# Where ScalarE issues the split of h that returns from device memory: behind the newest weight set's high part

## The chip, the cores and the metric

One NeuronCore of one Trainium2 chip runs the kernel. The metric is device time in microseconds (us); smaller is better. The engines are PE (TensorE, matrix products), ACT (ScalarE), DVE (VectorE), POOL (GpSimd) and SP (SyncE, which here only issues transfers). PEld is PE's loading of stationary operands.

## The reference

Two layers act on x of 256 positions by 1024 channels. Each layer is a half-step SwiGLU block, a mixing block of 16 heads in four groups, and another half-step SwiGLU block. A last RMSNorm follows.

```python
def swiglu(x, w_gate, w_up, w_down):
    return (jax.nn.silu(x @ w_gate) * (x @ w_up)) @ w_down     # 1024 -> 2816 -> 1024
...
x = x + 0.5 * swiglu(rms_norm(x, norm_ffn1[l]), ...)
x = x + hybrid_mixer(rms_norm(x, norm_mix[l]), ...)
x = x + 0.5 * swiglu(rms_norm(x, norm_ffn2[l]), ...)
```

The change touches only the SwiGLU blocks, four in all (called FFN below). There h stands for the 2816 values silu(gate) * up of each position.

## The kernel before, in words

**Sets.** All weights pass through the kernel as "sets", 328 of them, in one list: two blocks of 128 rows by up to 512 columns, 512 KB. `Set.load` issues the transfer into `wraw` on SP's queue (L137) and then calls `split`, which makes two tiles from it: `whi`, the rounded high part, by one ACT instruction, and `wlo`, the rest, by one DVE instruction that reads `whi`. Both are called through the helper `keep`, so the profile puts them on L115. A product in near-float32 precision takes six matmuls for each set and half of the positions (`Set.mm`, L149): high by high, high by low and low by high, for each of the two blocks.

**Order of work.** The 256 positions are two halves, h=0 and h=1. `consume(h, i)` uses set i for half h. The half h=1 follows five sets behind (LAG = 5), so that the traced order is (0,i), (1,i-5), (0,i+1), (1,i-4), and so on; at the end of a block the five outstanding uses of h=1 run alone (L773). `consume(0, i)` first loads sets up to i+2 (AHEAD = 2), so `done[0] - 1`, the newest loaded set, is i+2 from then on. The tiles `whi` and `wlo` have eight buffers each (`wsp`), so ACT may make `whi` of set j only when both halves have used set j-8. The raw tiles have four buffers, and each comes free when `wlo` is made.

**One FFN block.** The 2816 columns are cut into 11 chunks c of 256. Chunk c takes four sets (`gate_up`, s = 0 to 3), whose last one ends in `sg` = silu(gate) * up (L318 on ACT, L319 on DVE). From chunk 2 on, the two sets of `down_` for chunk c-2 come behind the four of chunk c. So a period is six sets. `down_` needs h transposed (`hT`), again as a high and a low part, `hhi` and `hlo`.

**Two ways to transpose.** For chunks 0, 1 and 10 (NEAR), `turn` transposes on PE. For the other eight chunks, `turn_far` transposes 32x32 blocks on DVE (L298), writes them to device memory in four transfers (L301) and reads them back with the blocks exchanged (L305), both on POOL's queue. Two yields place these steps: the read is traced four `advance` calls after `sg`, and `split` of the returned tile `pT` ten more. `advance` is called once for each `consume`, so `split` is traced in the fourteenth call. There are 8 chunks x 2 halves x 4 blocks = 64 such splits.

**Who sets the order on an engine.** The kernel is traced in the order above, and a planner then lays each engine's instructions into one fixed order, by what it expects to be ready when. Each engine works off its own order, one instruction after the other. `tc.issue_after(x)` makes what is traced in its block on x's engine stand behind x in that order; it adds no wait for x to finish, and it does nothing to other engines.

The names that follow: `Set.load` (L129 to L140), `split` (L119), `keep` (L111), `turn_far` (L294 to L309), `gate_up` (L311), `down_` (L322), `consume` (L748).

Of the kernel before, what the change touches and what calls it, by code (L numbers as in the profile page):

```python
# [11 lines left out]
AF = mybir.ActivationFunctionType  # L12
# [43 lines left out]
def hybrid_kernel(ctx: ExitStack, tc: tile.TileContext, a: dict, out: bass.AP):  # L56
    nc = tc.nc
# [12 lines left out]
    def bank(tag):  # L70
        return ps.tile([P, 512], F32, name=f"ps_{tag}")

    def quad(tag):
        return ps.tile([P, 4, P], F32, name=f"ps_{tag}")
# [36 lines left out]
    def keep(engine, f, *args, **kw):  # L111

        last = fixed.get(engine)
        with tc.issue_after(last.ins) if last is not None else nullcontext():
            ins = f(*args, **kw)  # L115
        if engine in fixed:
            fixed[engine] = ins

    def split(pt, hi, lo):  # L119
        keep("ACT", nc.scalar.activation, hi, pt, AF.Copy)  # L120
        keep("DVE", nc.vector.tensor_tensor, lo, pt, hi.bitcast(F32), op=ALU.subtract)

    class Set:

# [4 lines left out]
        def load(self, parts=1):  # L129

            n = self.n
            r = raw.tile([P, 2, 512], F32, name="wraw")[:, :, :n]
            self.hi = wsp.tile([P, 2, 512], F32R, name="whi")[:, :, :n]
            self.lo = wsp.tile([P, 2, 512], F32R, name="wlo")[:, :, :n]
            ks = [slice(2 * i // parts, 2 * (i + 1) // parts) for i in range(parts)]
            for k in ks:
                self.dma = nc.sync.dma_start(r[:, k], self.src[:, k])  # L137
            for k in ks:
                yield
                split(r[:, k], self.hi[:, k], self.lo[:, k])  # L140

        def mm(self, acc, hi, lo, first, last):
            xs = ((hi, self.hi), (hi, self.lo), (lo, self.hi))
# [18 lines left out]
    sets = []  # L162
# [6 lines left out]
    def spawn(gen):  # L169

        wait = next(gen, None)
        if wait is not None:
            alive.append([gen, wait])
# [5 lines left out]
    def advance():  # L179
        for job in list(alive):  # L180
            job[1] -= 1
            if job[1] <= 0:
                job[1] = next(job[0], None)
                if job[1] is None:
                    alive.remove(job)
        for h in range(2):
            for job in list(running[h]):
                job[1] -= 1
                if job[1] <= 0:
                    job[1] = next(job[0], None)  # L190
                    if job[1] == 0:
                        job[2] = True
                        job[1] = next(job[0], None)
                    if job[1] is None:
                        running[h].remove(job)
            if lines[h] and all(j[2] for j in running[h]):
                gen = lines[h].pop(0)
                running[h].append([gen, next(gen), False])
# [4 lines left out]
    class Norm:  # L203
# [33 lines left out]
        def take_turned(self, h, c, xg, parts=1, on=nc.sync):  # L237


            xg = xg.rearrange("p (k t) -> p k t", t=P)  # L240
            self.parts[h, c] = hi, lo = tuple(big.tile([P, 4, P], F32R, name=f"x{t}{h}{c}") for t in ("hi", "lo"))
            n = 4 // parts
            ks = [slice(n * i, n * i + n) for i in range(parts)]
            for k in ks:
                on.dma_start(xg[:, k], a["xT"][h, c, :, k])
            for k in ks:
                yield
                g = gcol[:, 4 * c:4 * c + 4][:, k].unsqueeze(2).to_broadcast([P, n, P])
                keep("DVE", nc.vector.tensor_tensor, xg[:, k], xg[:, k], g, op=ALU.mult)
                split(xg[:, k], hi[:, k], lo[:, k])  # L250
# [7 lines left out]
        def turn(self, h, c, xg):  # L258
            yield TURN_X
            pt = quad("t")  # L260
            for j in range(4):
                nc.tensor.transpose(pt[:, j, :], xg[:, j * P:(j + 1) * P], ident)  # L262
            hi, lo = (big.tile([P, 4, P], F32R, name=f"x{t}{h}{c}") for t in ("hi", "lo"))
            split(pt, hi, lo)
            self.parts[h, c] = hi, lo
# [7 lines left out]
    def residual(h, c, acc, scale, nxt):  # L273
        n = 2 if nxt.final and h == 1 and c == 1 else 1
        w = 512 // n
        for i in range(n):
            xs = x[h][:, c * 512 + i * w:c * 512 + i * w + w]
            nc.vector.scalar_tensor_tensor(xs, acc[:, i * w:i * w + w], scale, xs, op0=ALU.mult, op1=ALU.add)
            nxt.take(h, c, i, n)

    def add_ffn(norm, gu, down, nxt):
        phases.append(len(sets))
        hT = {}
        acc = {}

        def turn(h, c, hh):
            yield 2 if h == 1 and c == 10 else TURN_H
            pt = quad("t")
            for j in range(2):
                nc.tensor.transpose(pt[:, j, :], hh[:, j * P:(j + 1) * P], ident)  # L290
            hT[h, c] = tuple(hbuf.tile([P, 2, P], F32R, name=f"h{t}{h}") for t in ("hi", "lo"))
            split(pt[:, :2, :], *hT[h, c])

        def turn_far(h, c, hh):  # L294


            st = work.tile([P, 512], F32, name="z")[:, :256]
            nc.vector.transpose(st, hh)  # L298
            far = dram.tile([4, 32, 4, 64], F32, name="far")
            for a_ in range(4):  # L300
                nc.gpsimd.dma_start(far[:, :, a_, :].rearrange("b j e -> j b e"),  # L301
                                    st[32 * a_:32 * a_ + 32].rearrange("j (b e) -> j b e", b=4))
            yield FAR
            back = work.tile([P, 4, P], F32, name="pT").rearrange("p a t -> p (a t)")[:, :256]
            nc.gpsimd.dma_start(back, far.rearrange("b j a e -> (b j) (a e)"))  # L305
            yield BACK
            back = back.rearrange("p (a k i) -> p k a i", a=4, k=2)
            hT[h, c] = tuple(hbuf.tile([P, 2, P], F32R, name=f"h{t}{h}") for t in ("hi", "lo"))
            split(back, *(t.rearrange("p k (a i) -> p k a i", a=4) for t in hT[h, c]))  # L309

        def gate_up(h, c, s, st):  # L311
            if s == 0:
                acc[h] = bank("g")
            st.mm(acc[h], *norm.blocks(h, (2 * s, 2 * s + 1)), s == 0, s == 3)
            if s == 3:
                sg = work.tile([P, 256], F32, name="sg")
                r = norm.scale[h]
                nc.scalar.activation(sg, acc[h][:, :256], AF.Silu, scale=r)  # L318
                nc.vector.scalar_tensor_tensor(sg, acc[h][:, 256:], r, sg, op0=ALU.mult, op1=ALU.mult)  # L319
                spawn((turn if c in NEAR else turn_far)(h, c, sg))  # L320

        def down_(h, c, d, st):  # L322
            if c == 0:
                acc[h, d] = bank(f"d{h}")
            while (h, c) not in hT:
                advance()
            hi, lo = hT[h, c]
            st.mm(acc[h, d], [hi[:, k, :] for k in range(2)], [lo[:, k, :] for k in range(2)], c == 0, c == 10)
            if c == 10:
                residual(h, d, acc[h, d], 0.5, nxt)  # L330

        def add_down(c):
            for d in range(2):
                sets.append(Set(down[c, d], 512, lambda h, st, d=d: down_(h, c, d, st)))

        for c in range(11):
            for s in range(4):
                sets.append(Set(gu[c, s], 512, lambda h, st, c=c, s=s: gate_up(h, c, s, st)))
            if c > 1:
                add_down(c - 2)  # L340
        add_down(9)
        add_down(10)
# [418 lines left out]
    done = [0]  # L761
# [98 lines left out]
```

## Time and profile before

| what | value |
|---|---|
| three runs | 1020.0, 1019.18, 1019.8 us; median 1019.8 us |
| the profiled execution | 1020.97 us, of which the span from first to last instruction is 1019.2 us |
| PE, PEld busy | 996.3 us, 801.4 us |
| DVE, ACT busy | 642.0 us, 515.8 us |
| POOL busy | 195.0 us |
| transfers | 200.36 MB, mean 197 GB/s |
| granted clock of PE over the span | 0.995 |

How to read it: an engine that is busy nearly all the time sets the pace, and then the time that can be won is the time in which it stands still. A matmul's record covers more than the interval to the next one, since they are pipelined; the interval between two starts is what counts. Idle time of an engine that does not set the pace costs nothing by itself; the question is whether the pacing engine ever waits for it.

### The profile page before, as it was taken

The page shows a single profiled execution, that of the slowest core. Times are in us where ns is not written, and L with a number is a line of the kernel's source. Part 1 is how long each engine was busy: PE and PEld are TensorE (multiplying, and loading weights), DVE is VectorE, ACT ScalarE, POOL GpSimd, SP SyncE. Part 2 cuts the span into 40 slices and gives each one's busy share as a digit, 9 for nine tenths or more (in the row PEclk, how much of TensorE's full clock was granted, in tenths as well). Part 3 has the DMA queues.
Part 4 walks back from the last instruction along what each step waited for, and adds up shares of the span by engine and source line. Part 5 has one row for each costly group of instructions (what it writes and reads, how often), then busy time and mean ns, then how long its engine had stood idle before and what let it go on. Part 6 is the DMA issues. An engine that isn't in the chain of part 4 may idle for free.

```text
span 1019.2 us, 14178 instructions
## 1 busy us (share of the span) xinstructions
PE 996.3 (98%) x4899; PEld 801.4 (79%) x4899; DVE 642.0 (63%) x1223; ACT 515.8 (51%) x886; POOL 195.0 (19%) x351
## 2 busy tenths in 40 slices
PE   8999999999999999999999999999999999999997
PEld 5788787867778888788878888878678788888875
DVE  6565656786777456465755565648776775656464
ACT  6444444554665445354644454446466564445452
POOL 0132323010000023332102232310100001323230
PEclk9999999999999999999999999999999999999999
DMA  8677767644354466676656777755634455677671
GB/s 294 235 224 262 235 220 244 207 151 166 119 166 139 154 212 215 219 221 237 204 175 202 222 229 224 235 186 176 189 109 155 128 166 190 205 234 214 220 232 47
DMA packets 68855, 200.36 MB, mean 197 GB/s; under 512 B 12448, under 2 KB 20528, under 8 KB 68784
## 3 DMA queue, kind: packets, MB, share of 16 engines
q1 hardware_dynamic: 56352, 180.83, 55.1%
q0 software_dynamic: 11712, 17.86, 5.4%
q8 instruction: 38, 0.62, 0.3%
q10 hardware_dynamic: 720, 0.79, 0.2%
q14 instruction: 33, 0.27, 0.1%
HBM read 189.98 MB, written 9.45 MB: 196 GB/s over the span
## 4 chain that ended last, share of the span: by engine, by line
PE 40%; DMA 26%; DVE 11%; POOL 9%; issue 7%; ACT 7%; POOLq 0%; SPq 0%; ACTq 0%; DVEq 0%
PE ps_g L149 22%; DMA far<-z 13%; DMA pT<-far 11%; PE ps_d L149 10%; POOL far L301 9%; DVE wlo L115 5%; ACT whi L115 4%; PE ps_t L457 2%; DVE sg L319 2%; DMA wraw<-in_gu 1%; PE ps_t L445 1%; DVE z L298 1%; PE ps_d L399 1%; PE ps_t L379 1%; PE ps_t L262 1%
## 5 line engine op out<-in xcount | busy, mean ns | idle before, releaser
L115 DVE TENSOR_TENSOR wlo<-wraw,whi 128x1024 fp32r<-128x1024 f32 (+3 forms) x329 | 392.4, 1196 | 176.6 <-ACT whi L115 175.6
L115 ACT ACTIVATE whi<-wraw 128x1024 fp32r<-128x1024 f32 (+3 forms) x329 | 341.0, 1038 | 224.9 <-PE ps_g L149 105.4
L149 PE MATMUL ps_g<-whi,xhi 128*128 128x512 f32 (+2 forms) x896 | 352.0, 394 | 5.8 <-ACT whi L115 3.8
L149 PE MATMUL ps_g<-wlo,xhi 128*128 128x512 f32 (+2 forms) x896 | 347.5, 388 | 3.7 <-DVE wlo L115 3.6
L149 PE MATMUL ps_g<-whi,xlo 128*128 128x512 f32 (+2 forms) x896 | 346.4, 387 | 0.0
L149 PEld LDWEIGHTS ps_g<-whi,xhi 128*128 128x128 f32 x896 | 168.6, 188 | 47.5 <-ACT whi L115 6.7
L301 POOL DMA_DIRECT2D far<-z x256 | 139.8, 554 | 327.4 <-DVE z L298 322.8
L149 PEld LDWEIGHTS ps_g<-wlo,xhi 128*128 128x128 f32 x896 | 168.7, 188 | 37.3 <-DVE wlo L115 6.8
L149 PEld LDWEIGHTS ps_g<-whi,xlo 128*128 128x128 f32 x896 | 168.5, 188 | 31.7 <-DVE xlo L115 0.5
L149 PE MATMUL ps_d<-whi,hhi 128*128 128x512 f32 x352 | 138.9, 395 | 0.0
L149 PE MATMUL ps_d<-whi,hlo 128*128 128x512 f32 x352 | 137.8, 391 | 0.0
L149 PE MATMUL ps_d<-wlo,hhi 128*128 128x512 f32 x352 | 137.6, 391 | 0.0
L115 ACT ACTIVATE hhi<-pT 128x256 fp32r<-128x256 f32 x64 | 26.7, 417 | 153.4 <-DMA pT<-far 153.4
L115 DVE TENSOR_TENSOR hlo<-pT,hhi 128x256 fp32r<-128x256 f32 x64 | 27.2, 425 | 107.5 <-ACT hhi L115 107.4
L149 PEld LDWEIGHTS ps_d<-whi,hlo 128*128 128x128 f32 x352 | 66.4, 189 | 13.9
L149 PEld LDWEIGHTS ps_d<-wlo,hhi 128*128 128x128 f32 x352 | 66.6, 189 | 13.6
L149 PEld LDWEIGHTS ps_d<-whi,hhi 128*128 128x128 f32 x352 | 66.5, 189 | 13.4
L159 POOL TENSOR_TENSOR rstd<-ms,mhalf 128x1 f32<-128x1 f32 x14 | 8.6, 614 | 291.4 <-DVE ms L157 291.4
L305 POOL DMA_DIRECT2D pT<-far x64 | 35.6, 557 | 142.4 <-DMA far<-z 111.9
L318 ACT ACTIVATE sg<-ps_g,rstd 128x256 f32<-128x256 f32 x88 | 41.1, 467 | 22.4 <-PE ps_g L149 22.1
L319 DVE SCALAR_TENSOR_TENSOR sg<-ps_g,rstd,sg 128x256 f32<-128x256 f32 x88 | 42.1, 478 | 15.8 <-ACT sg L318 15.8
L416 ACT ACTIVATE p<-p,nm 128x128 f32<-128x128 f32 (+2 forms) x96 | 40.1, 419 | 22.8 <-DVE nm L408 10.5
(158 smaller groups left out, 654.4 us busy)
## 6 DMA issues: line engine op xcount, KB each, us to landing
wraw<-in_gu SPq DMA_DIRECT2D x175, 512.0 KB, 4.1
wraw<-in_down SPq DMA_DIRECT2D x88, 512.0 KB, 4.5
wraw<-in_win SPq DMA_DIRECT2D x24, 512.0 KB, 4.0
far<-z POOLq DMA_DIRECT2D x256, 32.0 KB, 4.0
pT<-far POOLq DMA_DIRECT2D x64, 128.0 KB, 3.7
wraw<-in_wout SPq DMA_DIRECT2D x16, 512.0 KB, 3.5
wraw<-in_win SPq DMA_DIRECT2D x16, 384.0 KB, 3.6
wraw<-in_w SPq DMA_DIRECT2D x8, 512.0 KB, 3.5
```

Of the source, the lines that this page charges most:

```text
L115: ins = f(*args, **kw)
L149: nc.tensor.matmul(acc, x_[k], w[:, k, :], start=first and i == 0, stop=last and i == 5)
L262: nc.tensor.transpose(pt[:, j, :], xg[:, j * P:(j + 1) * P], ident)
L298: nc.vector.transpose(st, hh)
L301: nc.gpsimd.dma_start(far[:, :, a_, :].rearrange("b j e -> j b e"), st[32 * a_:32 * a_ + 32].rearrange("j (b e) -> j b e", b=4))
L305: nc.gpsimd.dma_start(back, far.rearrange("b j a e -> (b j) (a e)"))
L318: nc.scalar.activation(sg, acc[h][:, :256], AF.Silu, scale=r)
L319: nc.vector.scalar_tensor_tensor(sg, acc[h][:, 256:], r, sg, op0=ALU.mult, op1=ALU.mult)
L379: nc.tensor.transpose(pt[:, j, :], z[:, j * P:(j + 1) * P], ident)
L399: nc.tensor.matmul(dst, qT[r, i // 2, :], keys(i)[r, :nk], start=True, stop=True)
L416: nc.scalar.activation(p[:, i, :], p[:, i, :], AF.Exp, bias=nm[:, i:i + 1], scale=-1.0, accum_out=den[:, i:i + 1])
L457: nc.tensor.matmul(o[64 * e:64 * e + 64, j, :], vals(2 * j + e, n), pts[n][:w, 2 * j + e, :], start=n == 0, stop=n == len(blocks) - 1)
```

## The change

`split` now returns the ACT instruction that makes the high part, `Set.load` keeps it as `self.last`, and `turn_far` traces its `split` inside `tc.issue_after` on the `last` of the newest loaded set. So the ACT instruction `hhi<-pT` stands behind `whi` of that set in ACT's order. The DVE instruction `hlo<-pT` gets no such tie; it still reads `hhi`. No instruction is added or removed, and no transfer changes.

```diff
@@ keep
         if engine in fixed:
             fixed[engine] = ins
+        return ins
 
     def split(pt, hi, lo):
-        keep("ACT", nc.scalar.activation, hi, pt, AF.Copy)
+        first = keep("ACT", nc.scalar.activation, hi, pt, AF.Copy)
         keep("DVE", nc.vector.tensor_tensor, lo, pt, hi.bitcast(F32), op=ALU.subtract)
+        return first
@@ Set.load
-                split(r[:, k], self.hi[:, k], self.lo[:, k])
+                self.last = split(r[:, k], self.hi[:, k], self.lo[:, k])
@@ turn_far
-            split(back, *(t.rearrange("p k (a i) -> p k a i", a=4) for t in hT[h, c]))
+            with tc.issue_after(sets[done[0] - 1].last.ins):
+                split(back, *(t.rearrange("p k (a i) -> p k a i", a=4) for t in hT[h, c]))
```

## Rows read from the trace of the kernel before

**Rows 1.** The page, part 1: busy us, share of the span, instructions.

```profile
PE 996.3 (98%) x4899; PEld 801.4 (79%) x4899; DVE 642.0 (63%) x1223; ACT 515.8 (51%) x886; POOL 195.0 (19%) x351
```

**Rows 2.** Chain of waits in order of time: start us, us, what.

```profile
354.87 1.36 PE ps_g L149 x6
```

**Rows 3.** Who waited for whom: us in total, times, longest us.

```profile
ACT hhi L115 <- DMA pT<-far: 153.4, 59, 6.6
```

**Rows 4.** Timeline of ACT, 408 to 419 us: start, us, instruction, [idle before <-releaser].

```profile
408.20 1.06 ACT L115 ACTIVATE whi<-wraw 128x1024 fp32r<-128x1024 f32 x1 [1.61 <-PE ps_g L149]
415.65 0.42 ACT L115 ACTIVATE hhi<-pT 128x256 fp32r<-128x256 f32 x1 [6.38 <-DMA pT<-far]
415.97 1.04 ACT L115 ACTIVATE whi<-wraw 128x1024 fp32r<-128x1024 f32 x1
416.92 0.40 ACT L115 ACTIVATE hhi<-pT 128x256 fp32r<-128x256 f32 x1
...
418.53 1.05 ACT L115 ACTIVATE whi<-wraw 128x1024 fp32r<-128x1024 f32 x1
```

**Rows 5.** Timeline of PE, six places: the matmuls that waited for a split weight.

```profile
102.52 0.50 PE L149 MATMUL ps_g<-wlo,xhi 128*128 128x512 f32 x1 [0.17 <-DVE wlo L115]
119.62 0.50 PE L149 MATMUL ps_g<-wlo,xhi 128*128 128x512 f32 x1 [0.44 <-DVE wlo L115]
168.82 0.50 PE L149 MATMUL ps_g<-whi,xhi 128*128 128x512 f32 x1 [0.18 <-ACT whi L115]
170.08 0.51 PE L149 MATMUL ps_g<-wlo,xhi 128*128 128x512 f32 x1 [0.76 <-DVE wlo L115]
417.06 0.49 PE L149 MATMUL ps_g<-whi,xhi 128*128 128x512 f32 x1 [0.74 <-ACT whi L115]
418.32 0.50 PE L149 MATMUL ps_g<-wlo,xhi 128*128 128x512 f32 x1 [0.76 <-DVE wlo L115]
669.29 0.50 PE L149 MATMUL ps_g<-whi,xhi 128*128 128x512 f32 x1 [0.93 <-ACT whi L115]
670.55 0.51 PE L149 MATMUL ps_g<-wlo,xhi 128*128 128x512 f32 x1 [0.76 <-DVE wlo L115]
969.17 0.50 PE L149 MATMUL ps_g<-wlo,xhi 128*128 128x512 f32 x1 [0.76 <-DVE wlo L115]
```

**Rows 6.** Groups by form: busy us, mean ns | idle us <-releasers.

```profile
L149 PE MATMUL ps_g<-whi,xlo 128*128 128x512 f32 x800 | 313.4, 392 | 0.0
L115 DVE TENSOR_TENSOR hlo<-pT,hhi 128x256 fp32r<-128x256 f32 x64 | 27.2, 425 | 107.5 <-ACT hhi L115 107.4
```

**Rows 7.** Timeline of ACT at the fourth of the six places.

```profile
660.24 1.06 ACT L115 ACTIVATE whi<-wraw 128x1024 fp32r<-128x1024 f32 x1 [1.61 <-PE ps_g L149]
...
668.20 1.04 ACT L115 ACTIVATE whi<-wraw 128x1024 fp32r<-128x1024 f32 x1
```

**Rows 8.** Stretches: PE, PEld, DVE, ACT, POOL busy (x), PEclk, DMA share, GB/s.

```profile
668.00:671.00 3.00, 1.31 (x5) 0.59 (x4) 2.16 (x4) 3.00 (x6) 0.00 (x0) 1.00 0.00 0
671.00:675.00 4.00, 4.00 (x13) 3.15 (x12) 3.31 (x5) 1.48 (x3) 1.87 (x4) 0.58 0.73 249
```

**Rows 9.** Timelines of ACT, PE and DVE at the second FFN block's end.

```profile
496.57 0.42 ACT L115 ACTIVATE hhi<-pT 128x256 fp32r<-128x256 f32 x1 [3.37 <-DMA pT<-far]
...
501.60 1.04 ACT L115 ACTIVATE whi<-wraw 128x1024 fp32r<-128x1024 f32 x1
...
505.40 0.39 PE L149 MATMUL ps_d<-whi,hhi 128*128 128x512 f32 x1
...
506.21 0.47 PE L149 MATMUL ps_d<-whi,hlo 128*128 128x512 f32 x1
...
504.98 0.68 DVE L228 TENSOR_TENSOR xn<-x,gain 128x512 f32<-128x512 f32 x1
...
506.13 1.22 DVE L115 TENSOR_TENSOR wlo<-wraw,whi 128x1024 fp32r<-128x1024 f32 x1
```

**Rows 10.** Instructions on the tile pT: us from a transfer's issue to its landing.

```profile
DMA to landing us min/median/max: 2.2/3.8/7.9
```

## The prediction

> **What bounds the kernel now.** I read the busy times first, then the waits, then the timelines of ACT and PE side by side where PE stands still. PE is busy 98% of the span, and no other engine over 63% [rows 1]. Six matmuls of 512 columns take 1.36 us from start to start, so PE's pace is 0.227 us each and a set costs 1.36 us per half, 2.72 us for both [rows 2]. PE sets the end, and only the time in which PE stands still can be won.
>
> The longest idle time that fits the change is ACT's: before `hhi<-pT` it stood 153.4 us, in 59 of the 64 splits, waiting for the read from device memory [rows 3]. That sum is not the gain. It is idle time of an engine that is half empty; what counts is how much of it PE feels.
>
> Rows 4 show one period, six sets long. The last `whi` in time starts at 408.20. Its successors wait for a buffer that PE frees every 2.72 us, so the next one was due at 410.92. But ACT's order has an `hhi` in front of it, whose data came at 415.65. So `whi` came at 415.97, 5.05 us late. PE's side is in rows 5: at 417.06 a matmul waited for that `whi`, at 418.32 one for its `wlo`. I work out a loss from the idle time shown: a record is 0.39 us long [rows 6] where the pace is 0.227, so a matmul behind a normal one lost its idle plus 0.16 us; behind a 0.50 us record it is idle plus 0.27 us. The pair lost 0.74 + 0.16 + 0.76 + 0.27 = 1.93 us. So PE swallowed 5.05 - 1.93 = 3.12 us of lateness before it stood. The place near 669 us gives the same: due at 660.24 + 2.72 = 662.96, came at 668.20 [rows 7], 5.24 late; lost 0.93 + 0.16 + 0.76 + 0.27 = 2.12, cover 3.12. The first of two splits of a period may be late by 3.1 us for nothing, and from there on PE pays one for one.
>
> **The change part by part.** *Where the split goes.* The fourteenth `advance` after `sg` of set i (chunk c of half 0, and the trailing chunk of half 1) falls beside use (0,i+6), when i+8 is the newest set. The two splits of a period therefore move behind `whi` of set i+8. In rows 4 the two stand in front of `whi` of i+6 (415.97) and of i+7, and i+8 is the one at 418.53. They move by three and two sets, to about 410.92 + 2 x 2.72 = 416.4 us plus one `whi` of 1.05, say 417.4 on an undisturbed clock. The second of them had no wait of its own at 416.92 [rows 4], so both data were there before 417.4. ACT's wait for the read should go almost wholly, in this, the second-worst period, and in the milder ones with more room.
>
> *What that frees.* Nine matmuls at six places waited for late weights [rows 5]. Idle: 0.17 + 0.44 + 0.18 + 0.76 + 0.74 + 0.76 + 0.93 + 0.76 + 0.76 = 5.50 us. Five stand behind a normal record, 5 x 0.16 = 0.8; four behind a long one, 4 x 0.27 = 1.1. Together 7.4 us. All six places are of the kind in rows 4. Nothing behind them is late: PE's input there is the weights alone, and the other waits in a period are ACT's own for buffers that PE frees, which is what an engine ahead of PE looks like.
>
> [...]
>
> *What is queued behind the tie.* Behind the moved pair on ACT stand `sg` of the next chunk and `whi` of i+9; the pair costs 0.42 + 0.40 us [rows 4]. This is beside the 3.1 us of cover, so I put it at nothing; without cover it would cost 0.8 x 32 = 26 us. On DVE the two `hlo` (0.43 each [rows 6]) come at the same time as `sg` and `wlo`; same cover, also nothing. `hT` itself is not needed for long: `down_` of chunk c is set i+13, and the split comes beside (0,i+6). Its buffers were last read at (0,i+2). POOL issues the next reads a period later, 16.3 us, so the later release of `pT` (by some 2 to 5 us) meets nobody. SP is passed by no transfer, but it profits: over 668 to 671 us the transfer engines were empty [rows 8], since raw buffers come free only through ACT and DVE.
>
> *Where the slack is short.* For half 1 of chunk 9 the fourteenth `advance` falls on the block's last set, and the newest set is the second one of the next phase. This occurs at three block ends (the fourth has no next phase). At the second one `hhi` moves from 496.57 to behind the `whi` at 501.60, so to 502.6 or some 0.6 to 1.4 later behind the norm's ACT work; PE reads it at 505.40 and `hlo` at 506.21 [rows 9]. DVE is busy with the residual and the norm until 504.98 + 0.68 = 505.66; then `hlo` ends at 506.1, just in time. If DVE's order puts one `wlo` of 1.22 us in front [rows 9], it is 1.1 us late. No row shows DVE's new order, so the cost of the three is between 0 and 3 x 1.1 = 3.3 us; a gain is excluded, since nothing at these ends waited for this split. The row nearest is the timely one; I take 0.3 us in all.
>
> *The sum.* Against the profiled execution's 1020.97 us (span 1019.2 and 1.8 around it): -7.4 - 1.7 + 0.3 = -8.8, so 1012.2. The median is 1.2 us under that execution. If this is the recording's cost, the median becomes 1019.8 - 8.8 = 1011.0; if it is the clock drop that the plain runs did not have, 1019.8 - 7.4 + 0.3 = 1012.7. I take the middle, 1011.8, with 1009.5 to 1014 as the forecast's own range (places a little more or less affected per run).
>
> **The rivals.** *A. Part is handed back at the block ends.* `hlo` behind one `wlo`, 1.1 us at each of three ends, and the norm behind it again as much: 3.3 to 4.4 us. Time 1011.8 + 3.3 = 1015, at most 1016. For it: the margin in rows 9 is 0.1 us. Against: 1.2 us of slack can be had by any small shift of DVE's order. Chance 0.10.
>
> *B. The same time.* Either the tie does not act, because ACT's order already has it so; rows 4 speak against this plainly, three `whi` stand behind the first `hhi`. Or the read comes later than now, as weight transfers no longer pause, and the stall returns behind `whi` of i+8. The worst second read landed by 416.92 in rows 4 (its `hhi` started without a wait), and with the new place at 417.4 and 3.1 of cover PE pays from 420.5, 3.6 us later. Reads took 3.8 us in the median and 7.9 at most [rows 10]; with 7.9 in place of a median one, 4.1 us longer, the worst period would lose 0.5 us, so all six places would have to grow by over 5 us to give back 7.4. [...] Time 1019 to 1020. Chance 0.06.
>
> *C. Slower.* One mechanism, at the three block ends: DVE's order, planned with expected times, puts `hlo` behind several of the next phase's `wlo` instead of one. Each costs 1.22 us; PE stands at the use of `hT` for half 1. From three such `wlo` at each end (3 x 3 x 1.22 = 11 us, less the 0.1 margin each) the loss passes the gain of 9: 1011.8 + 11 = 1023. Against it: the split is traced ahead of those loads, and is ready before they are. Chance 0.06.
>
> **How the numbers follow.** Forecast 0.78, A 0.10, B 0.06, C 0.06. The likeliest is 1011.8 us. The range takes the forecast's and most of A: 1009.0 to 1015.5; it leaves out the upper end of A, B and C, and a few hundredths below. A measurement of this kernel tells apart about 0.2%, 2 us: forecast and A are faster, 0.88; B is the same, 0.06; C slower, 0.06.
>
> **What would show it.** Right: ACT's wait for `pT<-far` falls from 153.4 us to under 15; in ACT's timeline both `hhi<-pT` of a period stand directly behind a `whi`, the one after two more than before; no matmul in the six places waits for `whi` or `wlo`; the clock stays at 1.00 near 671 us; DVE waits for ACT less. Wrong: PE waits at ps_d for `hlo` at the block ends near 190, 505 and 692 us (A, C), or ACT still stands before `hhi` for several us in each period (B). The prediction fails as a whole if the stalls in rows 5 stay while ACT's wait is gone: then late weights had another cause, such as late raw transfers.

## The result, and the profile after

The changed kernel took 1008.93 us in the median of 3 runs (1008.88 to 1009.02) against 1019.8 (1019.18 to 1020.0) before: a ratio of 0.9895, 95% interval 0.9872 to 0.9917. Run again later on another chip it took 1009.22 us (1008.77 to 1009.8) against 1020.41, ratio 0.9896 (0.9879 to 0.9914). So it is faster, by 10.9 us where 8.0 were forecast, and the first median lies 0.07 us below the lower end of the range. The profiled execution took 1008.93 us with a span of 1006.9, 12.3 us under the span before.

The page of the changed kernel, busy times (part 1) and the chain by engine (part 4):

```profile
PE 990.8 (98%) x4899; PEld 801.3 (80%) x4899; DVE 640.3 (64%) x1223; ACT 517.1 (51%) x886; POOL 195.6 (19%) x351
...
PE 89%; DVE 6%; ACT 3%; issue 1%; DMA 1%; POOLq 0%; SPq 0%; ACTq 0%; DVEq 0%
```

The busy times hardly differ from [rows 1], and nobody could read the gain from them. PE's share of the chain does show it. The same line of the kernel before:

```profile
PE 40%; DMA 26%; DVE 11%; POOL 9%; issue 7%; ACT 7%; POOLq 0%; SPq 0%; ACTq 0%; DVEq 0%
```

Before, the chain left PE again and again for the transfers (26%) and POOL (9%) and was on PE for 40% of the span; now it stays on PE for 89%.

Who waited for whom in the changed kernel (us in total, times, longest us):

```profile
DVE wlo L115 <- ACT whi L115: 248.9, 197, 1.8
ACT whi L115 <- PE ps_g L151: 212.9, 140, 3.5
...
PE ps_g L151 <- ACT whi L115: 2.1, 2, 1.6
...
PE ps_g L151 <- DVE wlo L115: 0.3, 1, 0.3
```

The line of [rows 3], ACT's 153.4 us before `hhi` for the read from device memory, is not there any more. ACT now waits for PE instead, 212.9 us before `whi` (105.4 before), which is an engine that has run ahead and finds no free buffer. What is left of PE's waits for split weights is at 5.7, 7.8 and 15.5 us, while the first weights come in.

ACT's timeline of the period that answers to [rows 4] (start, us, instruction, [idle before <-releaser]):

```profile
410.08 1.06 ACT L115 ACTIVATE whi<-wraw 128x1024 fp32r<-128x1024 f32 x1 [1.66 <-PE ps_g L151]
412.80 0.47 ACT L321 ACTIVATE sg<-ps_g,rstd 128x256 f32<-128x256 f32 x1 [1.66 <-PE ps_g L151]
413.17 1.05 ACT L115 ACTIVATE whi<-wraw 128x1024 fp32r<-128x1024 f32 x1
414.12 0.40 ACT L115 ACTIVATE hhi<-pT 128x256 fp32r<-128x256 f32 x1
414.42 0.46 ACT L321 ACTIVATE sg<-ps_g,rstd 128x256 f32<-128x256 f32 x1
414.78 0.41 ACT L115 ACTIVATE hhi<-pT 128x256 fp32r<-128x256 f32 x1
415.57 1.06 ACT L115 ACTIVATE whi<-wraw 128x1024 fp32r<-128x1024 f32 x1 [0.37 <-ACT hhi L115]
```

Both `hhi` stand behind one `whi`, with no idle time before either. So it is in all 28 periods with two of them; the eight that stand alone, at the beginnings and ends of the blocks, do not wait either. The next `whi` comes at its pace.

Stretches of the changed kernel (PE, PEld, DVE, ACT, POOL busy, PEclk, DMA share, GB/s):

```profile
100.00:200.00 100.00, 100.00 (x456) 83.07 (x455) 65.09 (x89) 50.90 (x73) 25.77 (x47) 1.00 0.71 227
400.00:500.00 100.00, 100.00 (x447) 82.56 (x446) 59.62 (x77) 48.62 (x67) 30.37 (x56) 1.00 0.73 225
...
660.00:680.00 20.00, 20.00 (x93) 16.34 (x92) 12.52 (x17) 10.17 (x17) 2.75 (x5) 1.00 0.62 194
```

PE has no gap in any of them. In the kernel before the same three had 98.46, 98.50 and 18.31 us of PE, the last at a clock of 0.91:

```profile
660.00:680.00 20.00, 18.31 (x73) 14.41 (x73) 8.83 (x11) 7.97 (x11) 3.87 (x7) 0.91 0.65 230
```

Where the 12.3 us came from I read from PE's two timelines, by the start of the same matmul (the n-th `ps_g<-wlo,xhi`) in both. The lead of the changed kernel grows in steps, and stands still in between to 0.1 us:

| place (us of the kernel before) | lead before and behind it | step | foreseen |
|---|---|---|---|
| first sets, to 36 | 0 to 0.87 | 0.87 | 0 |
| 102.5 and 119.6 | 0.87 to 2.10 | 1.23 | 0.93 |
| 169, 170 | 2.10 to 3.59 | 1.49 | 1.37 |
| 417, 418 | 3.57 to 5.63 | 2.06 | 1.93 |
| second block end, 496 to 524 | 5.63 to 7.03 | 1.40 | -0.1 |
| 669 to 675, clock included | 7.07 to 10.97 | 3.90 | 2.12 + 1.7 |
| second mixer, third block end | 10.97 to 10.67 | -0.30 | -0.1 |
| 969 | 10.67 to 12.01 | 1.34 | 1.03 |
| from there to the end | 12.01 to 12.3 | 0.3 | 0 |

### The profile page after: what moved, and what is told of

It reads as the page before. It is cut to its first block, busy times and chain, and to the rows that moved or that the text cites. A ratio compares the mean times of both kernels' runs of the same rounds, so it can differ in the third digit from the quotient of the medians.

```text
span 1006.9 us, 14176 instructions
## 1 busy us (share of the span) xinstructions
PE 990.8 (98%) x4899; PEld 801.3 (80%) x4899; DVE 640.3 (64%) x1223; ACT 517.1 (51%) x886; POOL 195.6 (19%) x351
## 4 chain that ended last, share of the span: by engine, by line
PE 89%; DVE 6%; ACT 3%; issue 1%; DMA 1%; POOLq 0%; SPq 0%; ACTq 0%; DVEq 0%
PE ps_g L151 54%; PE ps_d L151 28%; DVE wlo L115 2%; PE ps_t L460 2%; PE ps_t L448 1%; ACT whi L115 1%; PE ps_d L402 1%; DMA wraw<-in_gu 1%; PE ps_t L264 1%; PE ps_t L382 1%; ACT p L419 1%; PE ps_t L402 1%; ACT sq L155 1%; DVE blk L491 1%; PE ps_t L292 0%
## 5 line engine op out<-in xcount | busy, mean ns | idle before, releaser
L115 ACT ACTIVATE whi<-wraw 128x1024 fp32r<-128x1024 f32 (+3 forms) x329 | 342.2, 1041 | 320.4 <-PE ps_g L151 212.9
L300 DVE STREAM_TRANSPOSE z<-sg 128x256 f32<-128x256 f32 x64 | 28.4, 443 | 1.3
L155 ACT ACTIVATE sq<-x 128x512 bf16<-128x512 f32 (+1 forms) x29 | 17.6, 608 | 18.4 <-DVE x L280 18.3
```

What stands on the lines that cost most here:

```text
L155: nc.scalar.activation(sq[:, :sl.stop - sl.start], x[h][:, sl], AF.Square, scale=1.0 / 32.0, accum_out=stat)
```

## The experiments

**The theory**: `hhi` in front of the next `whi` in ACT's order makes weights late, and PE pays what passes 3.12 us. Rivals: DVE's order, in which `hlo` moved just as far, is what counts; the gain is in PE's order around the norm, which the planner changed a little as well; or any move of the split, however small, will do.

**The change cut in two by place.** `mid` leaves out half 1 of chunk 9 (the block ends), `ends` ties that alone.

```diff
-            with tc.issue_after(sets[done[0] - 1].last.ins):
+            with nullcontext() if (h, c) == (1, 9) else tc.issue_after(sets[done[0] - 1].last.ins):   # mid
+            with tc.issue_after(sets[done[0] - 1].last.ins) if (h, c) == (1, 9) else nullcontext():   # ends
```

> The tie for all returned splits but those of half 1 of chunk 9, the ones at the block ends. PE's planned order is then that of before, where the full change has the norm's transposes at the second block end behind a few more matmuls. Theory: the six stalls of PE came from weight splits queued behind hhi on ACT, 7.4 us of them, and the block end gave 1.4 us of its own (two PE waits near 501.7 and 516.8 us of before: 0.48 and 0.89). So 1008.9 + 1.4 = 1010.3 us, and those two waits are back. Rival 1, the block ends give nothing: 1008.9. Rival 2, the gain came from the planner's other moves and not from the tie in the periods: 1018 or more.

> The mirror image: the tie only for half 1 of chunk 9. PE's planned order is that of the full change; ACT's order in the periods is that of before. Theory: 1019.8 - 1.4 = 1018.4 us, ACT's wait for the read stays near 150 us, and the six stalls stay. Rival 1: 1019.8. Rival 2, PE's new order is what won the time: 1010 or less.

Measured on one chip: `mid` 1010.65 us (1009.6 to 1012.12), ratio 0.9923 (0.9902 to 0.9945); `ends` 1017.97 (1013.71 to 1019.3), 0.9987 (0.9971 to 1.0003). Waits, and a pair of stalled matmuls in PE's timeline, of `ends`:

```profile
ACT hhi L115 <- DMA pT<-far: 139.6, 55, 6.0
```

```profile
414.69 0.51 PE L151 MATMUL ps_g<-whi,xhi 128*128 128x512 f32 x1 [0.32 <-ACT whi L115]
415.95 0.50 PE L151 MATMUL ps_g<-wlo,xhi 128*128 128x512 f32 x1 [0.75 <-DVE wlo L115]
```

With the wait the stalls are there. `ends` has PE's whole order from the changed kernel, so that order alone isn't the gain. The other side is in PE's timeline of `mid`, the matmuls that turn the norm's last tile:

```profile
511.23 0.63 PE L264 MATMUL ps_t<-ident,xn 128*128 128x128 f32 x4 [0.44 <-DVE ms L159]
```

This wait is not in the changed kernel. To size it, `mid` and the changed kernel ran once more side by side.

> The changed kernel once more, as the mark for the three beside it on the same chip. Expected 1008.9 us, since it has hardly scattered so far (1008.88 to 1009.02). A rival by which the gain holds on one chip alone gives within 3 us of the kernel before.

> The tie everywhere but at the block ends (half 1 of chunk 9), now beside the changed kernel on one chip. If the tie at the block ends brings time, through PE's order around the norm (the matmul at 511 us that waited 0.44 us for the norm came back in the first run of this kernel, a loss of 0.6 us, and 1.7 us stood between the medians of two chips): 0.6 to 1.7 us above the changed kernel. If the block ends bring nothing, as the prediction's +0.3 us had it, it is level with the changed kernel or up to 0.5 us below.

`mid_b` took 1011.02 us (1010.86 to 1011.17), the changed kernel 1009.22: 1.8 us apart, in runs that do not overlap. The wait came back at the same place with 0.54 us. So the tie at the block ends is worth some 1.8 us, 0.1 above what was expected; of it the traces show 0.8 us at the second block end (by the lead over the kernel before, which grows by 1.4 there in `after_b` and by 0.6 in `mid_b`), and the spans of the two profiled executions (1009.0 and 1007.8) 1.2 in all.

**How far must the split go?** `tie3` and `tie2` tie it to an earlier `whi`.

```diff
-            with tc.issue_after(sets[done[0] - 1].last.ins):
+            with tc.issue_after(sets[done[0] - 3].last.ins):   # tie3
+            with tc.issue_after(sets[done[0] - 2].last.ins):   # tie2
```

> The tie goes to the set two older than the newest (i+6 in place of i+8). PE's order is that of before. Theory with its cover of 3.12 us: the first hhi stands behind whi of i+6, which is due at D; in the worst periods its data came at D + 5.1, so whi of i+7, due at D + 2.72, is 5.1 + 0.3 - 2.7 = 2.7 us late, inside the cover: no stall in the periods, time as with the full change less its block end, 1010.3 us, while ACT still waits some 60 to 100 us in all for the read. Rival, any waiting of ACT costs PE in proportion (half of the wait left, half of the gain): 1014 us. Rival, only the place behind i+8 helps: 1019.

> The tie goes to the set one older than the newest (i+7). Reading of the run with i+6: both returned splits then stand on ACT in front of one whi, so the later of the two reads counts, and whi came up to 5.55 us late where PE swallows 3.12. With i+7 the whi behind both is due 2.72 us later; the same worst read makes it 2.8 us late, inside the cover. So no PE wait in the periods, though ACT still stands before hhi now and then: 1009 to 1010.5 us. Rival, any wait of ACT before hhi costs PE: as ACT would still wait 20 us or more, 1013 or above.

`tie3` was a miss: 1021.6 us (1016.04 to 1028.5), ratio 1.0027 (1.0004 to 1.005). ACT's timeline and PE's in its worst period:

```profile
115.67 1.06 ACT L115 ACTIVATE whi<-wraw 128x1024 fp32r<-128x1024 f32 x1 [1.66 <-PE ps_g L151]
120.74 0.42 ACT L115 ACTIVATE hhi<-pT 128x256 fp32r<-128x256 f32 x1 [4.01 <-DMA pT<-far]
123.61 0.42 ACT L115 ACTIVATE hhi<-pT 128x256 fp32r<-128x256 f32 x1 [2.46 <-DMA pT<-far]
123.94 1.04 ACT L115 ACTIVATE whi<-wraw 128x1024 fp32r<-128x1024 f32 x1
```

```profile
125.03 0.50 PE L151 MATMUL ps_d<-whi,hhi 128*128 128x512 f32 x1 [1.24 <-ACT whi L115]
126.29 0.50 PE L151 MATMUL ps_d<-wlo,hhi 128*128 128x512 f32 x1 [0.76 <-DVE wlo L115]
```

I had counted the first read alone. Here both splits of a period stand in front of the same `whi`, and it is the second read, at 123.61, that sets its time. The `whi` was due at 115.67 + 2.72 = 118.39 and came 5.55 us late; PE lost 1.24 + 0.16 + 0.76 + 0.27 = 2.43, and 5.55 - 2.43 is 3.12 once more. So the law of the cover held in a kernel it was not made from, and the place was wrong.

```profile
ACT hhi L115 <- DMA pT<-far: 97.1, 47, 5.0
```

ACT's wait for the read was down from 153.4 to 97.1 us in total here, and the longest from 6.6 to 5.0 us [rows 3], and yet the kernel was no faster. Neither the sum nor the longest of an engine's waits tells what they cost; what counts is how late the work behind the waiter comes. By the intervals from start to start, PE waited at eight places of this trace, for `whi` that were 3.42 to 5.55 us late, and lost 11.7 us there; in the kernel before it waited at six, for `whi` 3.44 to 5.24 us late, and lost 7.6. At each of the fourteen, lateness less loss is 3.11 or 3.12 us. In the kernel before, the next latest `whi`, due at 894.42 + 2.72 = 897.14, came at 900.18, 3.04 us late, and PE did not wait.

`tie2`, with each split one `whi` further on, took 1009.01 us (1008.58 to 1010.15), ratio 0.9919 (0.9891 to 0.9947), level with the full change. ACT still waits a little for the read, and PE doesn't notice:

```profile
ACT hhi L115 <- DMA pT<-far: 10.8, 10, 2.5
```

The piece of ACT's timeline with the longest of these waits:

```profile
626.21 1.06 ACT L115 ACTIVATE whi<-wraw 128x1024 fp32r<-128x1024 f32 x1 [1.66 <-PE ps_g L151]
...
630.11 0.42 ACT L115 ACTIVATE hhi<-pT 128x256 fp32r<-128x256 f32 x1 [2.53 <-DMA pT<-far]
...
630.79 1.05 ACT L115 ACTIVATE whi<-wraw 128x1024 fp32r<-128x1024 f32 x1
```

The `whi` behind it was due at 626.21 + 2.72 = 628.93 and came 1.86 us late, the latest of this trace and well under the cover.

**DVE's order alone.** `dve_tie` ties `hlo` behind the newest `wlo` on DVE and leaves ACT's `hhi` where it was.

```diff
-        keep("DVE", nc.vector.tensor_tensor, lo, pt, hi.bitcast(F32), op=ALU.subtract)
+        return keep("DVE", nc.vector.tensor_tensor, lo, pt, hi.bitcast(F32), op=ALU.subtract)
```

> Only DVE's part is tied: hlo stands behind wlo of the newest set, hhi on ACT is where it was before. PE's order is that of the full change. Theory, ACT's order alone blocks: the six stalls stay, 1019.8 - 1.4 = 1018.4 us. Rival, the wait that matters is DVE's for hhi with wlo queued behind it (111.8 us in all before): the stalls go, 1009 to 1010 us.

1021.76 us (1021.24 to 1024.49), ratio 1.0034 (1.0017 to 1.0051). Waits of this kernel, and one of its stretches:

```profile
DVE wlo L115 <- ACT whi L115: 294.3, 182, 7.0
...
ACT hhi L115 <- DMA pT<-far: 162.2, 60, 6.9
```

```profile
671.00:675.00 4.00, 2.52 (x10) 1.87 (x11) 3.23 (x5) 3.71 (x6) 0.00 (x0) 1.00 0.26 72
```

The pair of stalls is there (PE busy 2.52 of 4 us), and `wlo` waits for `whi` 294.3 us in all: DVE's order alone brings nothing in the periods. The kernel was not 1.4 us faster than the one before, as expected, but slower. Its trace has six places again where PE waits, with the same cover of 3.11 or 3.12 us at each; they cost 8.9 us, where those of the kernel before cost 7.6. No run has ACT's tie together with DVE's order of before, so whether `hlo` had to move along is not shown.

This kernel has PE's and DVE's orders of the changed one, and its lead over the kernel before grows by 1.37 us across the second block end, as with the change (1.40). Of this, 0.4 us comes ahead of 503 us of the kernel before, and comes to `mid`, `mid_b` and `no_wait` (below) as well, which have PE's old order. They gain 0.70, 0.58 and 0.41 us across this block end. The other 0.7 to 1.0 us, then, goes with the two new orders and not with ACT's wait.

**The wait taken away.** `no_wait` is the kernel before with a split that reads the residual x, which is in its tile already; the turned h of these chunks is left out of the computation, so that no `hhi` waits for a read. All transfers are still issued.

```diff
-            back = back.rearrange("p (a k i) -> p k a i", a=4, k=2)
+            back = x[h][:, :256].rearrange("p (a k i) -> p k a i", a=4, k=2)
```

> The kernel before, without the tie; the returned split reads x, which lies in SBUF, in place of the tile that comes back, and so never waits. The writes to device memory and the reads back are still made, and their result is not used (this part of the output is left out). ACT, DVE and transfers do the same amount of work; PE's order is that of before. Theory: what cost PE is the wait for the read at that place in ACT's order, nothing else: 1010.3 us, like the tie without the block ends. Rival, the place of the split itself costs (0.42 us of ACT in front of whi, DVE crowded): 1014 or more.

1009.48 us (1008.65 to 1010.22), ratio 0.9919 (0.9888 to 0.995). ACT's timeline of one period:

```profile
402.36 0.42 ACT L115 ACTIVATE hhi<-x 128x256 fp32r<-128x256 f32 x1 [1.38 <-PE ps_d L149]
402.68 1.05 ACT L115 ACTIVATE whi<-wraw 128x1024 fp32r<-128x1024 f32 x1
403.71 0.42 ACT L115 ACTIVATE hhi<-x 128x256 fp32r<-128x256 f32 x1
```

The place was not kept. The planner laid 60 of the 64 splits two `whi` earlier than in the kernel before, and the other four one earlier. Each still stands in front of a `whi`, and ACT waits before 33 of them for a buffer that PE frees, 1.6 us at most, which PE does not feel. With the wait for the read gone, the gain in the periods comes without the tie: at the five rows of the table that hold the six places, the lead of `no_wait` grows by 1.23, 1.48, 2.06, 3.86 and 1.35 us, as that of the changed kernel does to within 0.04. Across the second block end it grows by 0.41 instead of 1.40. So a split in front of `whi` costs nothing here when it does not wait for a read, and what the tie brings in the periods is the freedom from that wait. That the very place of the kernel before would cost nothing without the wait is not shown.

**What may now be bought with the slack.** With ACT free, more of h can go through device memory in place of PE: the constant names the chunks that PE still turns.

```diff
-NEAR = (0, 1, 10)
+NEAR = (0, 10)   # near_0_10
+NEAR = (10,)     # near_10
```

> The full change, and chunk 1 too goes by way of device memory (NEAR = 0 and 10). That takes 2 transposes off PE for each half and block, 8 times; one such pair costs PE about 0.22 us where it stands between matmuls. With the tie the read has 3 us of cover and more, so nothing waits: 1008.9 - 1.8 = 1007.1 us. Rival, the earlier chunk is needed sooner than its read comes, or POOL's queue and the transfers at the block's start are in the way: 1009 or slower, with PE waiting at ps_d.

> The full change, and chunks 0 and 1 go by way of device memory (NEAR = 10 alone): 16 pairs of transposes less, 1008.9 - 3.5 = 1005.4 us. Chunk 0 is used nine sets after its sg instead of thirteen, so its split has two sets (5.4 us) of room for half 1 rather than six. Rival: chunk 0 comes too late and PE waits at ps_d at four block starts, some 1 to 3 us each: 1007 to 1015 us.

`near_0_10` took 1007.79 us, ratio 0.9905 (0.9874 to 0.9936). `near_10` was a miss: 1010.23 (1009.88 to 1010.36), 0.9927 (0.9903 to 0.9951). PE was done at 997.06, 2.9 us earlier than in the changed kernel, and the last output had landed by 1003.04. But then the program didn't end:

```profile
1000.00:1004.00 4.00, 0.00 (x0) 0.00 (x0) 0.20 (x1) 0.49 (x2) 0.00 (x0) 0.59 0.39 133
1004.00:1008.60 4.60, 0.00 (x0) 0.00 (x0) 0.00 (x0) 0.00 (x0) 0.00 (x0) 0.50 0.01 2
```

These are the last stretches of `near_10`. SP had drained at 1003.25, and POOL's first instruction of the program's end came at 1007.86. In between only some 8 KB moved (2 GB/s for 4.6 us), on a queue that the profile calls an instruction queue:

```profile
q14 instruction: 1, 0.01, 5.5%
```

My guess was a block of POOL's own instructions, and I put 64 small fills on POOL at the start to move the block's edge. Neither such a block nor its size is shown by a trace.

```diff
-    nc.gpsimd.memset(ph, 0.0)
+    nc.gpsimd.memset(ph, 0.0); pad = const.tile([P, 1], F32, name="pad"); [nc.gpsimd.memset(pad, 0.0) for _ in range(64)]
```

> The tie, chunks 0 and 1 of each half turned through device memory, and 64 one-column fills on GpSimd at the start of the program, while it has nothing else to do. Without the fills this kernel took 1010.23 us: PE was done 2.9 us earlier than in the changed kernel, but after the last output had landed (1003.04 us) and SP had drained (1003.25) GpSimd's first instruction of the program's end came only at 1007.86, with 8 KB moved on the transfer engines at 1004.0 to 1004.5 in between. Theory: GpSimd waited for a block of its own instructions; the fills move the block's edge by half a block, so the wait goes: end of the program about 1.2 us behind the drain as in the changed kernel, span 1004.5, time 1006.3. Rival: the wait belongs to GpSimd's queue with its 80 more transfers (a drain of it), and stays: 1010.2.

> The tie, and chunk 1 of each half turned through device memory too (40 more small transfers on GpSimd's queue, 16 fewer transposes on PE). First run on another chip 1007.79 us, where 16 transposes of half a pace each and their places in PE's order gave PE's last matmul 2.1 us earlier and the end of the program 1 us later than that. Expected 1.1 us below the changed kernel, 1007.8. The rival, that the difference was the chip: within 0.3 us.

`near_10_pad` took 1009.64 us (1008.73 to 1010.12): the wait stayed, SP drained at 1001.91 and POOL came at 1006.65, 4.7 us later. The expectation of 1006.3 failed. That the edge of a code block does it is not borne out; what POOL does in that time stays open. It goes with the number of transfers that POOL issues: 4.6 and 4.7 us with 408 of them, 1.4 with 368 (`near_0_10_b`, from SP's drain at 1003.02 to POOL at 1004.42), none that shows with 328. An instruction load is not ruled out by this. The last packet of 8 KB on that queue stands at 1004.25 in `near_10`, 3.6 us ahead of POOL, at 1003.16 in `near_10_pad`, 3.5 us ahead, and at 1004.02 in `near_0_10_b`, 0.4 us ahead, while the changed kernel has none from 928 us to the end of its span. Whose instructions they are the trace does not say.

With `near_0_10_b` what was expected came: 1007.51 us (1006.98 to 1007.88) beside 1009.22 for the changed kernel, 1.7 us under it and ratio 0.9879 (0.9862 to 0.9896) to the kernel before. It is the best of those run.

## Why the prediction was right, and where it was off

**PE's pace sets the end; only its stalls count.** Right: with ACT's 153.4 us gone, PE's busy time fell by 5.5 us and the time by 10.9. `tie3` shows the other half, with over a third of ACT's wait gone and nothing won.

**The law of lateness.** Shown, not only argued. The prediction had it from two places; the same working gives a cover of 3.11 or 3.12 us at six places of the kernel before, eight of `tie3` and six of `dve_tie`, for a lateness of 3.42 to 5.55 us. `tie2` showed ACT's waits that made `whi` late by less than that and cost nothing.

**Where the split goes.** Right: both behind `whi` of set i+8, at 414.1 to 415.2 us of a trace that is 3.6 to 5.6 us ahead there, against the 417.4 foreseen. The step that was right here is the one that I got wrong for `tie3`: which of two splits stands in front of which `whi`.

**What that frees.** The nine matmuls were sized at 7.4 us. The five rows of the table that hold the six places give 1.23 + 1.49 + 2.06 + (3.90 - 1.7) + 1.34 = 8.3. The stalls are the same; idle time plus a flat 0.16 or 0.27 us left out the neighbours that were stretched too (at 967.91 a matmul lost another 0.18 us with 0.02 of idle time shown). Start-to-start intervals would have had it.

**The clock.** The 1.7 us of the sum is (1 - 0.58) x 4.0 us, from the clock of 0.58 over 671 to 675 us in [rows 8]; that the plain runs lost it too is shown by no run. In the profiled execution it came back: the step at 669 to 675 was 3.90, foreseen 3.82, at a clock of 1.00. Whether the plain runs had the drop decided between 1011.0 and 1012.7, and that stays open. `ends` and `dve_tie` stalled at the same pair (666 and 672 us) and kept a clock of 1.00 over 660 to 680 us, as in the stretch of `dve_tie` shown above. `tie3` had the very stall of the kernel before at this pair (idle 0.93 and 0.76 us, at 679 us) at a clock of 1.00, and a drop behind its stall at 125 us instead:

```profile
127.00:131.00 4.00, 4.00 (x13) 3.10 (x12) 3.17 (x5) 1.00 (x2) 3.60 (x7) 0.57 0.84 243
```

So the drop did not come with the place: at this pair `ends`, `dve_tie` and `tie3` had none. Whether it comes again in a second execution of one kernel is not shown, since no kernel with these stalls was profiled twice. The three stretches of the changed kernel, without stalls, are at 1.00.

**What is queued behind the tie.** Costed at nothing, and nothing was lost: no PE wait in any period. The read got no slower, in the trace of the changed kernel:

```profile
DMA to landing us min/median/max: 2.3/3.8/7.5
```

With [rows 10] that is the same median and a shorter maximum, though the transfers no longer pause as in [rows 8]: over 661 to 664 us of the changed kernel, the stretch that answers to it, the transfer engines were busy for 0.63 of the time, at 191 GB/s.

**The block ends: the term that was mis-sized.** I took +0.3 us, between 0 and 3.3, and wrote that a gain is excluded, since nothing there waited for this split. It was -1.4 at the second of them. The split itself did as foreseen. ACT's, DVE's and PE's timelines there, against [rows 9]:

```profile
495.64 1.05 ACT L115 ACTIVATE whi<-wraw 128x1024 fp32r<-128x1024 f32 x1
496.59 0.58 ACT L115 ACTIVATE xhi<-ps_t 128x512 fp32r<-128x512 f32 x1
497.07 0.41 ACT L115 ACTIVATE hhi<-pT 128x256 fp32r<-128x256 f32 x1
```

```profile
498.91 0.68 DVE L230 TENSOR_TENSOR xn<-x,gain 128x512 f32<-128x512 f32 x1
499.51 0.15 DVE L159 SCALAR_TENSOR_TENSOR ms<-stat 128x1 f32<-128x1 f32 x1
499.58 0.42 DVE L115 TENSOR_TENSOR hlo<-pT,hhi 128x256 fp32r<-128x256 f32 x1
```

```profile
499.81 0.60 PE L264 MATMUL ps_t<-ident,xn 128*128 128x128 f32 x4
500.16 0.48 PE L151 MATMUL ps_d<-whi,hlo 128*128 128x512 f32 x1
```

With the lead of 6.1 us added, `hlo` ended at 506.1, as worked out, ahead of its use, and not behind a `wlo`. What I had not looked for is that the orders around the norm are planned as well, and change too. In the kernel before, two groups of the norm's transposes waited on PE, at 501.72 for `xn` (0.32 us) and at 516.83 for DVE's `xn` of 516.00, which is put down to `ms` (0.73):

```profile
501.72 0.66 PE L262 MATMUL ps_t<-ident,xn 128*128 128x128 f32 x4 [0.32 <-DVE xn L228]
...
516.83 0.63 PE L262 MATMUL ps_t<-ident,xn 128*128 128x128 f32 x4 [0.73 <-DVE ms L157]
```

DVE's timeline there, before:

```profile
515.40 0.69 DVE L115 TENSOR_TENSOR xlo<-ps_t,xhi 128x512 fp32r<-128x512 f32 x1 [1.09 <-ACT xhi L115]
516.00 0.68 DVE L228 TENSOR_TENSOR xn<-x,gain 128x512 f32<-128x512 f32 x1
516.60 0.15 DVE L157 SCALAR_TENSOR_TENSOR ms<-stat 128x1 f32<-128x1 f32 x1
```

and in the changed kernel:

```profile
508.31 0.69 DVE L230 TENSOR_TENSOR xn<-x,gain 128x512 f32<-128x512 f32 x1
509.96 0.69 DVE L115 TENSOR_TENSOR xlo<-ps_t,xhi 128x512 fp32r<-128x512 f32 x1 [0.96 <-ACT xhi L115]
510.57 0.15 DVE L159 SCALAR_TENSOR_TENSOR ms<-stat 128x1 f32<-128x1 f32 x1
```

The last `xn` now stands in front of an `xlo` that waits for ACT, and PE has the third group of transposes two matmuls later and the fourth two earlier; none waits. It is once more a waiter at the head of a strict order. `mid` and `mid_b`, without the tie at this place, keep the old order and the second of the two waits; `dve_tie`, with the new orders and without ACT's tie, keeps the gain. The first wait is gone in `mid`, `mid_b` and `no_wait` too, so 0.4 of the 1.40 us is not owed to the new orders, and its cause is open. So a gain was no more to be excluded than a loss where a planner reorders what follows.

**The start.** Another 0.87 us came in the first 36 us, where both kernels do the same. It is not the change: eight other profiled executions of the kernels above stood between 0.26 us behind and 1.29 ahead there, `ends` and `tie3` among them, which gained nothing.

**The median.** 1008.93 against 1011.8 is 2.9 us. If the plain runs gained what the profiled pair did, the block end gives 1.7 of it (-1.4 in place of +0.3) and the nine matmuls 0.9. The rest, 0.3 us, is within what the kernel before scatters.

**The rivals.** A (part handed back at the block ends) had the sign wrong. B did not occur in either form: the two `hhi` moved behind a later `whi`, and the reads took no longer than before (3.8 us in the median of both traces, 7.5 at most against 7.9). C did not occur: no `hlo` behind a `wlo` at the second block end, and no PE wait for one at any.

## What to carry to other kernels

An instruction that waits for a transfer, in the strict order of a half-empty engine, delays what stands behind it (here ACT, busy for 51%, stood up to 6.6 us before `hhi`, and `whi` came up to 5.24 us late); find what the bounding engine's buffers cover (here 3.12 us), and put the waiter behind the work that is needed sooner. Look in each period at how late the instruction behind the waiter comes, not at the sum of the waits nor at the longest. Where a planner writes the orders, a tie at one place moves others too: compare the orders, not only the tied instruction.

## What the runs showed of the hardware

- Three kernels in which `whi` stood behind a read from device memory scattered widely: the one before ran between 1014.23 and 1022.35 us beside these experiments, `ends` between 1013.71 and 1019.3, `tie3` between 1016.04 and 1028.5; the changed one, over both chips, ran between 1008.77 and 1009.8. Which periods passed the cover differed between two profiled executions: PE waited near 102, 120, 169, 417, 669 and 969 us in the kernel before, near 102, 415, 483, 666 and 981 us in `ends`, whose splits in the periods have the same places. But `dve_tie`, which waits as long, kept to 1021.24 to 1024.49, so that the reads make the scatter is not shown.
- At the end of the program POOL came late, long after its last work: 4.6 and 4.7 us behind SP's drain with 408 transfers issued from it, 1.4 with 368, none that shows with 328. One more chunk of each half through device memory put the end of PE's work 0.7 us earlier (`near_10` against `near_0_10`) and the end of the program 2.7 us later (spans 1008.6 and 1005.9). The reason is open.
- Behind a stall of PE the granted clock was lower in some profiled executions (0.58 over 671 to 675 us in [rows 8], behind 1.69 us without PE; 0.57 over 127 to 131 in `tie3`, behind 1.24 + 0.76 = 2.00 us) and not in others (`dve_tie`: 1.00 over 671 to 675, with PE busy for 2.52 of the 4 us; `ends`: 1.00 over 664 to 668, with 3.02).
